# Emptying a product's PSUM banks ahead of the next product's low parts, and eight banks in turn

## The chip, the cores and the metric

The kernel runs on one core of a Trainium2 chip. Its engines work side by side, each through its own queue in order: TensorE (PE in the profile; its weight loads are PEld), VectorE (DVE), ScalarE (ACT), GpSimd (POOL) and SyncE (SP), which here issues transfers. The metric is the device time of one execution in microseconds. Before the change three runs took 3308.37, 3308.54 and 3318.48 us.

## The reference

One decoder layer for a prompt of 512 tokens and 8 sample tokens (520 columns together), width 2048. Cut to the matrix products that matter here:

```
h   = modulate(rmsnorm(x, norm1_g), shift1, scale1)
rkv = h @ w_in                          # 2048 -> 6144, then attention and RWKV-7 on the halves
x   = x + gate1 * (concat(att, rwkv) @ w_out)              # 2048 -> 2048
h2  = modulate(rmsnorm(x, norm2_g), shift2, scale2)
gate, up = split(h2 @ w_gu)                                # 2048 -> 2 x 5632
x   = x + gate2 * ((silu(gate) * up) @ w_down)             # 5632 -> 2048
```

All of it is float32.

## The kernel before

**A product.** Every large matrix product is cut into products of 256 output rows. `product` (line 133) makes one of them with a seven-multiplication block scheme: for each pair of 128-row blocks of the input (a block of x, prepared once by `act_blocks`, line 109) it forms seven combinations of the four 128x128 weight blocks and multiplies them with seven combinations of the four blocks of x, and keeps seven sums M1 to M7. Each sum has 260 columns and fills one PSUM bank; the order of work is M1, M2, M6, M7, M4, M5, M3. There are eight banks. Seven belong to the seven sums by name, one each, so that M2 of a product must wait until M2 of the product before has been read; the eighth is for transposes.

**Float32 from two parts.** TensorE gets each operand as a high part, the value rounded to its fast 32-bit format, and a low part, the remainder. For each x block the weights go this way: SP loads them (line 130), two x blocks to a transfer pair and a buffer, with two such buffers (`RAW=2`); VectorE forms the combinations (lines 143 to 145, once for two x blocks); ScalarE casts the high part (line 149); VectorE subtracts it for the low part (line 150); TensorE does three matmuls for each of the seven sums: high by high, high by low, low by high (line 90, called by `mm`). These 21 matmuls on one x block are called a pass here. A product has eight passes in the input projection, the output projection, gate and up, and five or six in down. The high and low parts have three buffers (`HL=3`), so ScalarE can fill the fourth pass's only when TensorE is done with the first's.

**The sums.** `combine` (line 158) adds the seven banks up to the 256 x 520 result. ScalarE copies M1 (line 163), then VectorE adds M2 (line 164), M6 (165), M7 (166), subtracts M4 (167), adds M5 twice (168, 169) and M3 (170). A bank is free when its last reader is done.

**Stages.** The input projection and the mixers run to about 1471 us, the output projection (products o0 to o7) to 1708, gate and up (for u = 0 to 21 a gate product g and an up product u in turn, 44 in all) to 2715, and down to the end. After g comes a tanh (line 1419) and a product on VectorE (line 1420); after u a multiplication (1422) and a store to DRAM (1423). Down runs over four groups of 5, 6, 6 and 5 blocks; each reads the stored results back, prepares its x blocks and makes eight products (d00 to d07 for the first group), whose results are added to y on VectorE (lines 1440, 1445, 1446). In the last group the finished y is also transposed by TensorE through the eighth bank and stored.

**Order.** The program is traced in the order of the text. A planner then orders each engine's queue by a simulated timeline: of the instructions whose inputs and buffers it takes to be ready, the one traced first goes first. On the chip each engine follows that order, and waits where something is late.

Of the kernel before, what the change touches and what calls it, by code (L numbers as in the profile page):

```python
# [8 lines left out]
F32 = mybir.dt.float32  # L9
# [69 lines left out]
def hymba_step(tc, a):  # L79
# [17 lines left out]

    def strassen(mkpool, sfx, ht, NX=8, RAW=2, HL=3, PC=2, PT=1, S4="ps", placed=None):
        wf, xp, tp, sm_, pt_ = placed or [mkpool(n + sfx) for n in ("wts", "x", "tmp")] + [None, None]
        sm_, pt_, turn_ = sm_ or tp, pt_ or tp, [0]  # L100
        psF, psG = mkpool("ps" + sfx, space=PSUM, side="left"), mkpool("px" + sfx, space=PSUM, side="right")

        def psf(name, tag="ps"):
            return (psG if tag == "ps" else psF).tile([P, 512], F32, tag=tag, name=name, bufs=1)

# [67 lines left out]
        return tp, wf, xp, psF, psf, pair_tile, act_blocks, columns, product, combine  # L173

    from contextlib import ExitStack

    with ExitStack() as top:
# [19 lines left out]
        def tr(out, in_, n=P):  # L197
            pe.transpose(out, in_=in_, identity=ident[:n, 0:n])  # L198
# [67 lines left out]
        pha = mid.enter_context(ExitStack())  # L266
        tp, wf, xp, psF, psf, pair_tile, act_blocks, columns, product, combine = strassen(lambda name, **kw: pools(pha)(name, **{"side": RIGHT, **kw}), "a", HS, PC=3)

# [560 lines left out]
        with ExitStack() as wk_stack:  # L829
# [497 lines left out]


        yp, xC, pt_, tmp_, xA, sB, wts_, xB, xD = [pool(n + "f") for n in ("y", "xc", "pt", "tmp", "xa", "small", "wts", "xb", "xd")]
        xpool = (xA, xA, xB, xB, xC, xC, xC, xD)  # L1330
        tp, wf, xp, psF, psf, pair_tile, act_blocks, columns, product, combine = strassen(
            pool, "f", HT, placed=(wts_, xpool, tmp_, sB, pt_), PT=2, S4="pt")
        NRAW = NRAWF
# [47 lines left out]
        nt = [slice(b * P, min(b * P + P, TOK)) for b in range(5)]  # L1381
        po = psF.tile([P, 512], F32, tag="M1", name="n2", bufs=1)
        for b, t_ in enumerate(nt):
# [8 lines left out]
        ve.tensor_tensor(rd, ident.unsqueeze(1).to_broadcast([P, 5, P]), rt[:, 1].unsqueeze(2).to_broadcast([P, 5, P]), op=ALU.mult)  # L1392
        rs2 = [psF.tile([P, 512], F32, tag=order[1 + i], name=f"rs2{i}", bufs=1) for i in range(2)]
        mm(rs2[0], ones, rd[:, :4].rearrange("p b t -> p (b t)"))
# [31 lines left out]
        YD = 2  # L1426
        for gi, (p0, p1) in enumerate(groups):
# [6 lines left out]
            for u in range(KT // 2):  # L1434
                c = combine(product(columns(w_down[:, u * 256 : (u + 1) * 256]), kp, xs, f"d{gi}{u}"), f"d{gi}{u}")
                f2 = slice(2 * u, 2 * u + 2)
                for j in range(2):
                    f = 2 * u + j
                    if j < YD:
                        ve.scalar_tensor_tensor(y[:, f, :SEQ], in0=c[:, j, :SEQ], scalar=modT[:, 48 + f, 0:1], in1=y[:, f, :SEQ],  # L1440
                                                op0=ALU.mult, op1=ALU.add)
                    else:
                        ac.mul(c[:, j, :SEQ], c[:, j, :SEQ], modT[:, 48 + f, 0:1])
                        gp.tensor_add(y[:, f, :SEQ], y[:, f, :SEQ], c[:, j, :SEQ])
                ve.tensor_mul(c[:, :, SEQ:], c[:, :, SEQ:], modT[:, 48 + 2 * u : 50 + 2 * u, 1:9])
                ve.tensor_add(y[:, f2, SEQ:], y[:, f2, SEQ:], c[:, :, SEQ:])
                if gi == len(groups) - 1:
                    ot = pair_tile(f"ot{u}", "pt").rearrange("p a t -> p (a t)")[:, :1024].rearrange("p (b c) -> p b c", b=4)
                    for j in range(2):
                        f = 2 * u + j  # L1450
                        pt = psf(f"pyt{f}")
                        for b in range(4):
                            tr(pt[:, b * 128 : (b + 1) * 128], y[:, f, b * 128 : (b + 1) * 128])
                        ac.copy(ot[:, :, j * 128 : (j + 1) * 128], pt.rearrange("p (b e) -> p b e", b=4))
                    sp.dma_start(a["y_prompt"][0].rearrange("(b p) d -> p b d", p=P)[:, :, u * 256 : (u + 1) * 256], ot)
        ys = [pair_tile(f"ys{i}").rearrange("p a t -> p (a t)")[:NB, :1024] for i in range(2)]
        for i in range(4):
            pt = psF.tile([P, 512], F32, tag=order[i], name=f"pys{i}", bufs=1)
            for j in range(4):
# [34 lines left out]
```

## Time and profile before

| | |
|---|---|
| median of three runs | 3308.54 us (3308.37 to 3318.48) |
| the profiled execution | 3317.61 us, its span 3315.8 us |
| TensorE busy (matmuls / weight loads) | 2895.7 / 2576.9 us |
| VectorE busy | 2486.4 us |
| ScalarE busy | 1275.8 us |
| GpSimd busy | 203.5 us |
| mean granted TensorE clock | 0.915 of full speed |
| transfers | 476.19 MB |

The span is from the first to the last instruction of the profiled execution. Busy times are unions of the instructions' durations; matmuls overlap one another, so a busy TensorE is not one at its peak. The share of a whole span hides the stages, which have different limits.

### The profile page before, as it was taken

How to read it: one execution, taken by the hardware profiler on the slowest of the kernel's cores; microseconds unless marked ns; L12 is line 12 of the kernel's file. 1: busy time of each engine (PE TensorE's matmuls, PEld its weight loads, DVE VectorE, ACT ScalarE, POOL GpSimd, SP SyncE). 2: the span in 40 equal slices, each digit the busy share in tenths (PEclk: the TensorE clock that was granted, in tenths of full speed). 3: DMA queues.
4: the chain of work that ended last, by engine and by line, in shares of the span. 5: the costliest groups of instructions: out<-in, count | busy, mean ns of one | idle time of the engine just before them, and what ended most of it. 6: DMA issues, size and time to landing. Idle time of an engine off the chain costs nothing.

```text
span 3315.8 us, 59346 instructions
## 1 busy us (share of the span) xinstructions
PE 2895.7 (87%) x23474; PEld 2576.9 (78%) x23474; DVE 2486.4 (75%) x4888; ACT 1275.8 (38%) x2047; POOL 203.5 (6%) x216
## 2 busy tenths in 40 slices
PE   6798999789979699868959999999999987888988
PEld 3577888688946466648859999999999987887887
DVE  6866788777757576657787878777777788889886
ACT  3443443333424244543443333333333343334333
POOL 0100111110010221110000000000000000000000
PEclk8889999889968798869979999999999999999989
DMA  8656666544389895443313333333333332323223
GB/s 272 228 179 211 191 209 199 181 134 135 116 258 295 243 256 136 117 121 109 109 38 99 112 109 109 109 109 103 109 103 115 103 131 93 111 88 115 90 96 103
DMA packets 460443, 476.19 MB, mean 144 GB/s; under 512 B 83070, under 2 KB 384083, under 8 KB 460164
## 3 DMA queue, kind: packets, MB, share of 16 engines
q1 hardware_dynamic: 449984, 452.15, 43.7%
q10 hardware_dynamic: 7428, 11.65, 1.1%
q0 software_dynamic: 2752, 8.60, 0.8%
q8 instruction: 184, 3.01, 0.4%
q14 instruction: 95, 0.78, 0.1%
HBM read 409.10 MB, written 68.17 MB: 144 GB/s over the span
## 4 chain that ended last, share of the span: by engine, by line
DVE 21%; PE 19%; DMA 17%; ACT 4%; issue 4%; SPq 2%; POOL 0%; ACTq 0%; DVEq 0%; POOLq 0%
DMA raw_ada<-in_ada_w 1%; SPq L130 1%; DMA K<-in_cache_k 1%; DVE x_a L125 1%; DMA a<-actd 1%; PE pz L90 1%; PE u15M L90 1%; PE g1M L90 1%; PE ada L90 1%; PE u14M L90 1%; PE u10M L90 1%; PE g17M L90 1%; PE u11M L90 1%; PE g6M L90 1%; PE g2M L90 1%
## 5 line engine op out<-in xcount | busy, mean ns | idle before, releaser
L90 PE MATMUL ada<-raw_ada,c_st 128*32 128x512 f32 x448 | 80.9, 760 | 24.4 <-DMA raw_ada<-in_ada_w 23.8
L1266 POOL TENSOR_TENSOR K<-K,qb 128x1024 f32<-128x1024 f32 (+2 forms) x24 | 58.5, 2447 | 125.4 <-DMA K<-in_cache_k 99.9
L1217 ACT ACTIVATE z<-z,mx 128x128 f32<-128x128 f32 (+3 forms) x64 | 35.8, 559 | 74.6 <-DVE mx L1216 37.8
L1066 ACT ACTIVATE Sall<-pch,ppl 64x64 f32<-64x64 f32 x128 | 39.4, 308 | 57.4 <-PE pch L90 52.6
L90 PEld LDWEIGHTS pg<-AR,BK 64*128 64x128 f32 x256 | 41.5, 238 | 23.4 <-DVE GM L925 8.1
L90 PE MATMUL pg<-AR,BK 64*128 64x128 f32 x256 | 50.1, 344 | 10.2 <-DVE GM L925 6.3
L90 PE MATMUL pz<-ak,aq 64*128 64x256 f32 (+3 forms) x128 | 56.0, 565 | 3.4 <-DVE at L1235 2.9
L198 PE MATMUL pzt<-ident,z 128*128 128x128 f32 x160 | 36.6, 334 | 20.2 <-ACT z L1219 15.6
L1213 DVE SCALAR_TENSOR_TENSOR z<-pz,rnq,T 128x128 f32<-128x128 f32 (+3 forms) x64 | 34.6, 543 | 23.9 <-PE pz L90 22.7
L90 PE MATMUL g0M<-x_g,g0hl 128*128 128x260 f32 x168 | 33.7, 369 | 19.4 <-ACT x_g L124 6.4
L198 PEld LDWEIGHTS pzt<-ident,z 128*128 128x128 f32 x160 | 20.6, 162 | 37.6 <-ACT z L1219 18.2
L90 PEld LDWEIGHTS ada<-raw_ada,c_st 128*32 128x32 f32 x448 | 11.0, 120 | 49.8 <-DMA raw_ada<-in_ada_w 37.7
L90 PE MATMUL o0M<-x_m,o0hl 128*128 128x260 f32 x168 | 32.5, 360 | 18.1 <-ACT x_m L124 14.4
L90 PEld LDWEIGHTS g0M<-x_g,g0hl 128*128 128x128 f32 x168 | 30.0, 263 | 23.0 <-ACT x_g L124 7.7
L90 PEld LDWEIGHTS o0M<-x_m,o0hl 128*128 128x128 f32 x168 | 29.0, 254 | 21.8 <-ACT x_m L124 17.0
L1440 DVE SCALAR_TENSOR_TENSOR y<-c_d,modT,y 128x512 f32<-128x512 f32 x64 | 45.7, 748 | 0.0
L925 DVE TENSOR_TENSOR GM<-pg,cst 128x512 f32<-128x512 f32 x32 | 21.9, 685 | 31.3 <-PE pg L90 31.2
L90 PE MATMUL ao<-adr,c_st 128*32 128x256 f32 x384 | 31.7, 402 | 14.5 <-DMA adr<-in_ada_w 11.1
L1267 DVE TENSOR_REDUCE lg<-K 128x16 f32<-128x1024 f32 (+2 forms) x24 | 29.1, 1213 | 20.4 <-POOL K L1266 20.3
L90 PE MATMUL ada<-xb,c_st 128*32 128x512 f32 x128 | 22.0, 765 | 25.2 <-DMA xb<-in_ada_w 19.9
L90 PE MATMUL po<-zt,av 128*64 128x128 f32 x320 | 40.7, 314 | 0.4 <-ACT zt L1229 0.3
L1219 ACT ACTIVATE z<-z,mx 128x128 f32<-128x128 f32 (+3 forms) x64 | 35.5, 560 | 9.6 <-DVE mx L1218 8.9
(2111 smaller groups left out, 9087.8 us busy)
## 6 DMA issues: line engine op xcount, KB each, us to landing
raw_ada<-in_ada_w SPq DMA_DIRECT2D x56, 1024.0 KB
adr<-in_ada_w SPq DMA_DIRECT2D x48, 512.0 KB
xb<-in_ada_w SPq DMA_DIRECT2D x16, 1024.0 KB
actd<-c_u SPq DMA_DIRECT2D x22, 520.0 KB
a<-actd SPq DMA_DIRECT2D x22, 520.0 KB
lsd<-lx SPq DMA_DIRECT2D x12, 520.0 KB
prd<-rkv SPq DMA_DIRECT2D x24, 256.0 KB
K<-in_cache_k SPq DMA_DIRECT2D x16, 384.0 KB
```

The costliest lines, as they stand in the source:

```text
L90: pe.matmul(out, lhsT=lhsT, rhs=rhs, start=start, stop=stop)
L125: ve.tensor_sub(x[:, 1, o:e], src, x[:, 0, o:e].bitcast(F32))
L130: sp.dma_start(raw.rearrange("p (k m) c -> p k (m c)", k=2), src[k * P : (k + 2) * P, :].rearrange("(k p) m -> p k m", p=P))
L198: pe.transpose(out, in_=in_, identity=ident[:n, 0:n])
L925: ve.tensor_tensor(GM[i][:, :, :, h], pg, gmask.unsqueeze(2).to_broadcast([P, 2, 2, P]), op=ALU.mult)
L1066: ac.activation(S[hb[h], ch + 1, hb[h]], pc_[hb[h], ch, :], AF.Copy, scale=ppl[hb[h], pr, ch : ch + 1])
L1213: ve.scalar_tensor_tensor(z, in0=pzs[h][:, :nk], scalar=rn[:, qi, h : h + 1], in1=Ts[h][:, 384 - 128 * qi :], op0=ALU.mult, op1=ALU.add)
L1217: ac.activation(z, z, AF.Exp, bias=mx[:, 0:1], accum_out=mx[:, 1:2])
L1219: ac.activation(z, z, AF.Copy, scale=mx[:, 2:3])
L1266: OK.tensor_mul(K[:n], K[:n], qb[:n])
L1267: ve.tensor_reduce(lg[:n, i, :], K[:n].rearrange("p (g e) -> p g e", e=E), axis=AX.X, op=ALU.add)
L1440: ve.scalar_tensor_tensor(y[:, f, :SEQ], in0=c[:, j, :SEQ], scalar=modT[:, 48 + f, 0:1], in1=y[:, f, :SEQ], op0=ALU.mult, op1=ALU.add)
```

## The change

It has three parts. In every product the low parts of the second and third x block (i = 1 and 2) are queued on VectorE behind the last sum of the product that was combined before (`tc.issue_after`: order of issue alone, no waiting for its end). From the second normalization on, all PSUM tiles come from one pool of eight banks with one name, taken in turn, so that a product's M1 gets the bank that its predecessor did not use; the pools of the output projection are closed for that. And the VectorE work behind a product in gate, up and down (lines 1420, 1422 with its store, and down's additions with the last group's transposes) is collected in a list `after` and traced behind the second x block of the next product. The branch for `j >= YD`, which was never taken, is dropped.

```diff
-        psF, psG = mkpool("ps" + sfx, space=PSUM, side="left"), mkpool("px" + sfx, space=PSUM, side="right")
+        psF, psG = (ppool or mkpool)("ps" + sfx, space=PSUM, side="left"), (ppool or mkpool)("px" + sfx, space=PSUM, side="right")
+
+        ring = []
 
         def psf(name, tag="ps"):
+            if ring:
+                return ring[0].tile([P, 512], F32, tag="m", name=name, bufs=8)
             return (psG if tag == "ps" else psF).tile([P, 512], F32, tag=tag, name=name, bufs=1)
...
+        held, after = [None], []
+
         def product(load, kpairs, xs, name, hook=None):
 
+            prev, held[0] = held[0], None
             M = {m: psf(f"{name}{m}", m) for m in order}
...
                     ac.copy(w[:, 0], tw[:, j, 1:])
-                    ve.tensor_sub(w[:, 1], tw[:, j, 1:], w[:, 0].bitcast(F32))
+
+                    with tc.issue_after(prev) if i in (1, 2) and prev is not None else nullcontext():
+                        ve.tensor_sub(w[:, 1], tw[:, j, 1:], w[:, 0].bitcast(F32))
                     for m in order:
...
                     if hook:
                         hook()
+                    while i == 1 and after:
+                        after.pop(0)()
             return M
...
-            ve.tensor_add(q[1, 1], q[1, 1], v["M3"])
+            held[0] = ve.tensor_add(q[1, 1], q[1, 1], v["M3"]).ins
             return c
...
+        ps_out.close()
+        ring.append(pool("ring", space=PSUM))
+        po = psf("n2")
...
-            ve.scalar_tensor_tensor(g, in0=th, scalar=1.0, in1=g, op0=ALU.add, op1=ALU.mult)
+
+            def gate(g=g, th=th):
+                ve.scalar_tensor_tensor(g, in0=th, scalar=1.0, in1=g, op0=ALU.add, op1=ALU.mult)
+
+            after.append(gate)
             v = combine(product(columns(w_gu[:, DFF + u * 256 : DFF + (u + 1) * 256]), kp_g, xs, f"u{u}", hook=fill_f(1)), f"u{u}")
-            ve.tensor_mul(v, v, g)
-            sp.dma_start(actd[u], v)
+
+            def gated(u=u, g=g, v=v):
+                ve.tensor_mul(v, v, g)
+                sp.dma_start(actd[u], v)
+
+            after.append(gated)
+        while after:
+            after.pop(0)()
...
+                def add(gi=gi, u=u, c=c):
+                    f2 = slice(2 * u, 2 * u + 2)
+                    for f in (2 * u, 2 * u + 1):
+                        ve.scalar_tensor_tensor(y[:, f, :SEQ], in0=c[:, f % 2, :SEQ], scalar=modT[:, 48 + f, 0:1], in1=y[:, f, :SEQ],
                                                 op0=ALU.mult, op1=ALU.add)
+                    ve.tensor_mul(c[:, :, SEQ:], c[:, :, SEQ:], modT[:, 48 + 2 * u : 50 + 2 * u, 1:9])
+                    ve.tensor_add(y[:, f2, SEQ:], y[:, f2, SEQ:], c[:, :, SEQ:])
...
+                after.append(add)
+        while after:
+            after.pop(0)()
```

## Rows read from the trace of the kernel before

**Rows 1.** Stretches: us; busy us and instructions by engine; clock; DMA share; GB/s.
```profile
core 0: us, PE busy (x) PEld busy (x) DVE busy (x) ACT busy (x) POOL busy (x), PEclk, DMA share, GB/s
60.00:1471.00 1411.00, 1227.97 (x10768) 988.42 (x10764) 970.75 (x2184) 559.67 (x1128) 186.57 (x185) 0.87 0.63 190
...
1777.70:2715.50 937.80, 881.97 (x7060) 859.85 (x7058) 737.01 (x1195) 343.61 (x407) 0.00 (x0) 0.99 0.34 109
2715.50:3315.80 600.30, 511.58 (x3776) 486.03 (x3776) 498.74 (x956) 216.38 (x284) 0.00 (x0) 0.94 0.31 101
...
1757.60:1777.70 20.10, 20.10 (x171) 20.10 (x170) 16.57 (x28) 8.59 (x10) 0.00 (x0) 1.00 0.33 103
```

**Rows 2.** Line 90 on TensorE, 1777.7 to 2715.5: idle us, times, by ender.
```profile
  DVE c_u L164: 18.5, 21
  DVE c_g L164: 18.2, 21
  ACT u21hl L149: 2.5, 1
```

**Rows 3.** Chain of waits, 1990 to 2030: start us, us, what.
```profile
1995.71 3.69 DMA g6w<-in_w_gu
...
1999.50 0.06 DVE g6w L143
...
2000.11 0.43 DVE c_u L164
...
2000.59 17.14 PE g6M L90 x141
```

**Rows 4.** Timeline at u5 to g6: start us, us, instruction, [idle before].
```profile
1996.75 2.09 DVE L150 TENSOR_TENSOR g6hl<-g6w,g6hl 128x896 fp32r<-128x896 f32 x2 [1.14 <-ACT g6hl L149]
...
1997.67 0.38 ACT L163 COPY c_u<-u5M 128x260 f32<-128x260 f32 x1
...
1998.19 1.09 PE L90 MATMUL g6M<-x_g,g6hl 128*128 128x260 f32 x6
1999.50 0.69 DVE L143 TENSOR_TENSOR g6w<-g6w 128x512 f32<-128x512 f32 x1 [0.66 <-DMA g6w<-in_w_gu]
2000.11 0.42 DVE L164 TENSOR_TENSOR c_u<-c_u,u5M 128x260 f32<-128x260 f32 x1
...
2000.59 15.69 PE L90 MATMUL g6M<-x_g,g6hl 128*128 128x260 f32 x129 [1.30 <-DVE c_u L164]
...
2003.77 1.08 DVE L150 TENSOR_TENSOR g6hl<-g6w,g6hl 128x896 fp32r<-128x896 f32 x1
...
2005.11 1.24 DVE L1422 TENSOR_TENSOR c_u<-c_u,c_g 128x1040 f32<-128x1040 f32 x1
...
2006.30 2.62 ACT L149 CAST g6hl<-g6w 128x896 fp32r<-128x896 f32 x3 [3.32 <-PE g6M L90]
```

**Rows 5.** Timeline at g0 to u0.
```profile
1757.57 0.43 DVE L164 TENSOR_TENSOR c_g<-c_g,g0M 128x260 f32<-128x260 f32 x1
...
1757.68 7.00 PE L90 MATMUL u0M<-x_g,u0hl 128*128 128x260 f32 x57
1757.91 0.42 DVE L165 TENSOR_TENSOR c_g<-c_g,g0M 128x260 f32<-128x260 f32 x1
1758.25 0.69 DVE L143 TENSOR_TENSOR u0w<-u0w 128x512 f32<-128x512 f32 x1
...
1761.62 0.42 DVE L170 TENSOR_TENSOR c_g<-c_g,g0M 128x260 f32<-128x260 f32 x1
```

**Rows 6.** The chain of waits in down, 2957 to 2995.
```profile
2960.06 6.43 PE d15M L90 x51
...
2967.53 3.11 DVE d15hl L150 x3
...
2971.07 3.50 DMA d16w<-in_w_down
...
2975.28 0.42 DVE c_d L164
```

More of the change, by code (lines that the diff above doesn't have):

```diff
@@ L96, in hymba_step, with strassen @@
     xsel = dict(M1=0, M2=1, M3=2, M4=6, M5=3, M6=4, M7=5)
-    def strassen(mkpool, sfx, ht, NX=8, RAW=2, HL=3, PC=2, PT=1, S4="ps", placed=None):
+    def strassen(mkpool, sfx, ht, NX=8, RAW=2, HL=3, PC=2, PT=1, S4="ps", placed=None, ppool=None):
         wf, xp, tp, sm_, pt_ = placed or [mkpool(n + sfx) for n in ("wts", "x", "tmp")] + [None, None]
         sm_, pt_, turn_ = sm_ or tp, pt_ or tp, [0]
-        psF, psG = mkpool("ps" + sfx, space=PSUM, side="left"), mkpool("px" + sfx, space=PSUM, side="right")
+        psF, psG = (ppool or mkpool)("ps" + sfx, space=PSUM, side="left"), (ppool or mkpool)("px" + sfx, space=PSUM, side="right")
+        ring = []
         def psf(name, tag="ps"):
+            if ring:
+                return ring[0].tile([P, 512], F32, tag="m", name=name, bufs=8)
             return (psG if tag == "ps" else psF).tile([P, 512], F32, tag=tag, name=name, bufs=1)
@@ L169, in combine @@
             ve.tensor_add(q[0, 1], q[0, 1], v["M5"])
-            ve.tensor_add(q[1, 1], q[1, 1], v["M3"])
+            held[0] = ve.tensor_add(q[1, 1], q[1, 1], v["M3"]).ins
             return c
-        return tp, wf, xp, psF, psf, pair_tile, act_blocks, columns, product, combine
-    from contextlib import ExitStack
+        return tp, wf, xp, psF, psf, pair_tile, act_blocks, columns, product, combine, after, ring
+    from contextlib import ExitStack, nullcontext
     with ExitStack() as top:
@@ L266, in hymba_step @@
         pha = mid.enter_context(ExitStack())
-        tp, wf, xp, psF, psf, pair_tile, act_blocks, columns, product, combine = strassen(lambda name, **kw: pools(pha)(name, **{"side": RIGHT, **kw}), "a", HS, PC=3)
+        tp, wf, xp, psF, psf, pair_tile, act_blocks, columns, product, combine, after, ring = strassen(lambda name, **kw: pools(pha)(name, **{"side": RIGHT, **kw}), "a", HS, PC=3)
         pp_ = pools(pha)("par")
@@ L1326, in hymba_step @@
         mid.close()
+        ps_out = top.enter_context(ExitStack())
         yp, xC, pt_, tmp_, xA, sB, wts_, xB, xD = [pool(n + "f") for n in ("y", "xc", "pt", "tmp", "xa", "small", "wts", "xb", "xd")]
         xpool = (xA, xA, xB, xB, xC, xC, xC, xD)
-        tp, wf, xp, psF, psf, pair_tile, act_blocks, columns, product, combine = strassen(
-            pool, "f", HT, placed=(wts_, xpool, tmp_, sB, pt_), PT=2, S4="pt")
+        tp, wf, xp, psF, psf, pair_tile, act_blocks, columns, product, combine, after, ring = strassen(
+            pool, "f", HT, placed=(wts_, xpool, tmp_, sB, pt_), PT=2, S4="pt", ppool=pools(ps_out))
         NRAW = NRAWF
@@ L1381, in hymba_step @@
         nt = [slice(b * P, min(b * P + P, TOK)) for b in range(5)]
-        po = psF.tile([P, 512], F32, tag="M1", name="n2", bufs=1)
+        ps_out.close()
+        ring.append(pool("ring", space=PSUM))
+        po = psf("n2")
         for b, t_ in enumerate(nt):
@@ L1392, in hymba_step @@
         ve.tensor_tensor(rd, ident.unsqueeze(1).to_broadcast([P, 5, P]), rt[:, 1].unsqueeze(2).to_broadcast([P, 5, P]), op=ALU.mult)
-        rs2 = [psF.tile([P, 512], F32, tag=order[1 + i], name=f"rs2{i}", bufs=1) for i in range(2)]
+        rs2 = [psf(f"rs2{i}") for i in range(2)]
         mm(rs2[0], ones, rd[:, :4].rearrange("p b t -> p (b t)"))
@@ L1435, in hymba_step @@
                 c = combine(product(columns(w_down[:, u * 256 : (u + 1) * 256]), kp, xs, f"d{gi}{u}"), f"d{gi}{u}")
[L1436 to L1440, printed above, removed]
-                                                op0=ALU.mult, op1=ALU.add)
-                    else:
-                        ac.mul(c[:, j, :SEQ], c[:, j, :SEQ], modT[:, 48 + f, 0:1])
-                        gp.tensor_add(y[:, f, :SEQ], y[:, f, :SEQ], c[:, j, :SEQ])
@@ L1445, in hymba_step @@
[L1445 to L1455, printed above, removed]
+                def add(gi=gi, u=u, c=c):
+                    f2 = slice(2 * u, 2 * u + 2)
+                    for f in (2 * u, 2 * u + 1):
+                        ve.scalar_tensor_tensor(y[:, f, :SEQ], in0=c[:, f % 2, :SEQ], scalar=modT[:, 48 + f, 0:1], in1=y[:, f, :SEQ],
+                                                op0=ALU.mult, op1=ALU.add)
+                    ve.tensor_mul(c[:, :, SEQ:], c[:, :, SEQ:], modT[:, 48 + 2 * u : 50 + 2 * u, 1:9])
+                    ve.tensor_add(y[:, f2, SEQ:], y[:, f2, SEQ:], c[:, :, SEQ:])
+                    if gi == len(groups) - 1:
+                        ot = pair_tile(f"ot{u}", "pt").rearrange("p a t -> p (a t)")[:, :1024].rearrange("p (b c) -> p b c", b=4)
+                        for j in range(2):
+                            f = 2 * u + j
+                            pt = psf(f"pyt{f}")
+                            for b in range(4):
+                                tr(pt[:, b * 128 : (b + 1) * 128], y[:, f, b * 128 : (b + 1) * 128])
+                            ac.copy(ot[:, :, j * 128 : (j + 1) * 128], pt.rearrange("p (b e) -> p b e", b=4))
+                        sp.dma_start(a["y_prompt"][0].rearrange("(b p) d -> p b d", p=P)[:, :, u * 256 : (u + 1) * 256], ot)
@@ L1456, in hymba_step @@
+                after.append(add)
+        while after:
+            after.pop(0)()
         ys = [pair_tile(f"ys{i}").rearrange("p a t -> p (a t)")[:NB, :1024] for i in range(2)]
         for i in range(4):
-            pt = psF.tile([P, 512], F32, tag=order[i], name=f"pys{i}", bufs=1)
+            pt = psf(f"pys{i}")
             for j in range(4):
```

1 line of the change is left out of this document (removed).

## The prediction

> **What bounds the kernel now.** I read the stretches first. The change touches every product of the kernel, but most of it lies in gate and up and in down, which are 937.8 and 600.3 us of the 3315.8 us span [rows 1]. In gate and up TensorE is busy 882.0 of 937.8 us and VectorE 737.0; in down it is 511.6 and 498.7 of 600.3, so there the two engines are about level. What an undisturbed product takes is also in that group: u0, which the trace shows without a pause, needs 20.10 us, that is 0.1196 us for each of its 168 matmuls. The 42 products g1 to u21 at that pace would take 42 x 20.10 = 844 us; they take 937.8, so 94 us are lost, 2.23 us a product.
>
> Next, what ended TensorE's idle time there. In each of the 42 products one wait ends with the sum of line 164: 18.5 + 18.2 = 36.7 us [rows 2]. The largest wait for a high part (line 149) is 2.5 us, in u21. Idle time understates the loss, since it counts from the modelled end of the last matmul. In g6 six matmuls start at 1998.19; at 0.12 us each the seventh would start at 1998.91, but starts at 2000.59 [rows 4], 1.68 us late against 1.30 us of idle time shown. With 0.38 us added for each of 42, the wait costs 36.7 + 16.0 = 52.7 us.
>
> The chain of waits says what is behind line 164: a weight transfer of 3.69 us, line 143 on it, line 164, and then TensorE [rows 3]. The timeline tells it as VectorE's queue [rows 4]. The seven sums of u5 could begin at 1998.05, when ScalarE has copied M1 (line 163, 1997.67 + 0.38). But ahead of them VectorE has two low parts of g6 (line 150, 2.09 us from 1996.75), then waits 0.66 us for the transfer that line 143 needs, then does line 143. Line 164 starts at 2000.11, 1.92 us after g6's first matmul, and its bank is the one M2 of g6 writes. The six matmuls that ran before it are M1 of the first pass and M1 of the second, drawn ahead because no other bank was free. A pass is the 21 matmuls on one block of x, 2.51 us.
>
> That has a second effect. With two passes interleaved, the first ends late, so ScalarE gets a buffer for the fourth high part only at 2006.30, 8.1 us after the product began and after 3.32 us of idle time ended by TensorE [rows 4]. From that follow the low parts, the release of the weight buffer, the next transfer of 3.7 us, and line 143 of the next boundary: a loop that closes on itself in about 21.5 us.
>
> **The change part by part.** *The order.* The low parts of the second and third pass (i = 1 and 2) issue after the seventh sum of the product before; that of the first pass stays free. It adds no instruction. Behind the held-back low part stands TensorE: in its plain order the second pass needs the low part after 21 + 2 matmuls, 23 x 0.1196 = 2.75 us after the product begins. If the planner draws the 14 matmuls of the second pass that use high parts alone ahead, 37 matmuls or 4.4 us; with the third pass's too, 6.1 us.
>
> When is it there? Line 164 follows line 165 by 0.34 us in u0 [rows 5], so seven sums take 2.35 us bare; u0 shows them with lines 143 to 145 between them, 1757.57 to 1761.95, 4.4 us. The low part adds about 1.05 (half of 2.09 in [rows 4]). If line 164 starts 0.1 us ahead of the product's first matmul, as in u0, the low part is ready at 3.3 to 5.35 us; against a need at 4.4 that costs 0 to 1.0 us. If line 164 still stands behind line 143 and its transfer and starts at 1.92 as now, it is ready at 5.3 to 7.4. I take a start in the middle, at 0.5, and the low part at 3.9 to 5.95 us, so 0 to 1.6 us and 0.8 in the middle. This takes the place of 1.68. The bounds of this term are 0 and 2.6 us a product (5.3 against a need at 2.75).
>
> *The ring.* M1 of the next product takes the eighth bank, M2 the bank of M1 (free once line 163 has copied it), M6 that of M2, and so on. M6 is needed 0.72 us after the start and each next bank 0.36 us later, while the sums free one each 0.34 us: with VectorE on time, TensorE no longer waits for a bank, and the passes need not be interleaved, which shortens the loop above. What u0 shows with seven banks is the lower bound: sums from -0.11 us on, the transfer of line 143 long there, 57 matmuls without a break [rows 5], the whole product 20.10 us. So 20.10 + 0.8 + 0.3 (0.3 for the waits for high parts, which stay; an estimate, five times u21's 2.5 us over 42 products) = 21.2 a product, 890 us in all, and 47 us gained. Both ends: 20.4 a product gives 81 gained; 20.1 + 2.6 + 0.3 = 23.0 gives 28 lost.
>
> The Trainium skill speaks against the ring. "TensorE: Matmul & The Clock Gate", in its section on HAM oscillation, reports a kernel where a second set of PSUM buffers "gave no further gain", and the section after it a kernel that cycles through the banks and loses clock between groups. By the first the ring alone would be worth nothing; by the second it would cost clock. The trace agrees with neither so far as it goes: the 42 pauses at banks here cost time while the granted clock is 0.99 [rows 1].
>
> *The deferred work.* The product gate (line 1420) and the multiply (line 1422, 1.24 us [rows 4]) move behind the second pass of the next product, and with them the store of line 1423 on SP's queue; down's four additions to y move likewise. Nothing reads the results within a product: the store of u is read only in down, y only at the end. I cost this at 0; VectorE's spare time hides it (737 of 937.8 busy). If that cover is gone, it is 1.24 us in front of line 143 of the second weight pair, once in each product.
>
> *Down.* The same order and ring. Its chain goes through 51 matmuls (6.43 us), a high part, three low parts (3.11), a transfer (3.50) and then line 164 [rows 6]; the ring lets the first pass end sooner, which shortens the first link. VectorE's 498.7 busy us are the floor, so at most 101.6 can be won. Against that, the second low part now comes after line 170: if TensorE waits for one more low part in each product it is 32 x 1.05 = 34 lost. I take 0.3 us a product, 10 gained, nearer to nothing since VectorE is nearly full.
>
> *Earlier stages.* The order also holds for the 24 products of the input projection and the 8 of the output projection, which have no ring. TensorE needs the sums there first anyway, so at most one low part is late or one sooner at each boundary: 31 x 1.05 = 33 us either way. I take 0.2 us lost each, 6 us.
>
> *The sum.* 47 + 10 - 6 = 51 us. From the profiled execution's 3317.6 us that leaves 3266.6. The median of the runs is 3308.5, 9.1 us below that execution, so the forecast is 3257.5, rounded to **3258**.
>
> **The rivals.**
> *The wait changes its name.* TensorE's pause moves from line 164 to the second pass's low part, about 1.7 us as before, because VectorE has the same work in the same 6 us. For it: VectorE is busy without a break from 1999.50 to the low part at 2003.77 [rows 4]. Against it: a fifth of VectorE's time is free and u0 shows room. Then down and the rest cancel, too: 3300 to 3317, about 3308.
>
> *VectorE sits on line 143 with everything behind it (slower).* The planner saw line 143 ready before line 164 (that is the order now). With the low part barred, line 143 and its two followers come straight after the first low part, and VectorE waits there for the transfer. Line 164 starts at 1.92 as before, but the low part at 4.3 or later, ready at 5.3: 2.55 us against the 1.68 lost now, 0.87 x 42 = 37, and 6 more from the earlier stages: 3352. It decides from the point where the transfer lands later than some 0.7 us after the product's start; now line 143 starts 1.31 after it in g6. Against it: with the first pass ending sooner the transfer is issued sooner.
>
> *The clock falls.* If handing banks round made the clock of gate and up what down has now, 0.94 for 0.99 [rows 1], TensorE would lose 5% of 938 us, 47 us: 3355 with nothing gained. The pauses get shorter, not longer, so this is unlikely. It is the Trainium skill's second case above.
>
> *u0's pace everywhere.* 81 us in gate and up and 1 us a product in down, 32: 113 less, 3195.
>
> **How the numbers follow.** The forecast 0.55, its own range 3230 to 3290; the wait that changes its name 0.17; VectorE on line 143 0.16; the clock 0.03; u0's pace 0.09. This kernel's runs tell 0.3%, about 10 us, from no change. Faster by more than that: 0.55 + 0.09 + 0.02 of the second case = 0.66; within it 0.13; slower 0.16 + 0.03 + 0.02 = 0.21. The range that leaves out 2 in 10 reaches from most of the fast case to a little past the unchanged one: 3205 to 3325.
>
> **What would show it.** In the changed profile line 164's share of TensorE's idle time in gate and up should fall from 36.7 us to under 10, and waits for line 150 rise to some 20 to 30. On VectorE at a boundary the seven sums stand before the second low part; line 164 starts within 0.7 us of the product's first matmul. The first pass ends before 6 us, and the idle time before line 143 shrinks. Gate and up should be near 890 us, down near 590, the part to 1471 us within some 20 us of its length. I am wrong if line 164 still starts 1.5 us late, if the wait for line 150 takes 1.7 us or more in a product, or if the gain in gate and up is lost in the first 1471 us.

## The result, and the profile after

The changed kernel takes 3407.07 us (median of 4 runs, 3394.28 to 3412.40) against 3313.51 us for the kernel before on the same chip (3308.37 to 3322.96): a ratio of 1.027 [1.024, 1.030]. It is slower by some 94 us, where 51 us faster was forecast. The rival named as the slower one came about, and with it a second cost that no case held: the low part that was held back also holds a weight buffer.

In the changed file VectorE's combinations are lines 150 to 152 (143 to 145 before), the high cast 156 (149), the low part 159 (150), the copy of M1 174 (163), the seven sums 175 to 181 (164 to 170), the product gate 1437, the multiply 1443, and SP's load 134 (130).

The stretches of the changed kernel, with the columns of [rows 1]:

```profile
core 0: us, PE busy (x) PEld busy (x) DVE busy (x) ACT busy (x) POOL busy (x), PEclk, DMA share, GB/s
60.00:1489.00 1429.00, 1238.68 (x10768) 991.16 (x10764) 970.59 (x2183) 558.31 (x1128) 191.01 (x185) 0.86 0.62 188
...
1797.80:2786.70 988.90, 902.53 (x7058) 866.69 (x7057) 743.46 (x1192) 340.06 (x406) 0.00 (x0) 0.99 0.32 103
2786.70:3404.00 617.30, 514.72 (x3779) 484.32 (x3777) 501.12 (x960) 217.24 (x286) 0.00 (x0) 0.95 0.30 98
```

Against [rows 1], gate and up went from 937.8 to 988.9 us, down from 600.3 to 617.3, and the output projection begins at 1490 us in place of 1472. That is 51 + 17 + 18, and 2 between them: the 88 us by which the span grew. VectorE's work did not grow (737 to 743 us in gate and up) and the clock there is 0.99 as before. So time was lost in waiting.

TensorE's idle time in gate and up by what ended it, the answer to [rows 2] (us, times; the largest groups):

```profile
  DVE c_g L175: 9.8, 19
  ACT c_g L174: 9.6, 18
  ACT u21hl L156: 2.7, 1
  DVE g14hl L159: 2.5, 2
```

The wait for the first sum fell, from 36.7 us to 9.8 for the sums of gate products and almost none for those of up. A wait for ScalarE's copy of M1 came, since with the ring M2 takes the bank that this copy frees; ring and deferral without the order show no such wait, so the ring by itself does not bring it. The rest is spread over single products' high and low parts, so I added it up by place. For the 42 products I took each pair of successive matmuls of a product that start more than 0.15 us apart and counted what exceeds 0.118 us, by the pass in which the late matmul stands (by its number, 21 to a pass). What a lower clock adds is counted with the waits. The last row is an experiment of the next section, the changed kernel without the order:

| us over 42 products | 1st pass | 2nd | 3rd | 5th | 7th | gate and up |
|---|---|---|---|---|---|---|
| before | 68.9 | 3.1 | 0 | 0 | 16.1 | 937.8 |
| after | 65.6 | 26.8 | 0 | 48.4 | 2.1 | 988.9 |
| ring and deferral alone | 4.9 | 2.6 | 19.1 | 0 | 34.8 | 905.2 |

Against the kernel before, the first two passes lose 92 us where they lost 72, and the fifth, which is the first to use the third pair of weights, loses 48 where it lost nothing. In the seventh 14 us come back. Against the same kernel without the order the picture is another: the order costs 85 us in the first two passes and 48 in the fifth, and 52 come back in the third and seventh. What ring and deferral had won in the first two passes, the order took away again.

The timeline of the changed kernel at u5 to g6, the boundary of [rows 4] (start us, us, instruction, idle before):

```profile
2029.81 0.65 PE L90 MATMUL g6M<-x_g,g6hl 128*128 128x260 f32 x4
2031.01 0.69 DVE L150 TENSOR_TENSOR g6w<-g6w 128x512 f32<-128x512 f32 x1 [3.38 <-DMA g6w<-in_w_gu]
2031.62 1.08 DVE L159 TENSOR_TENSOR g6hl<-g6w,g6hl 128x896 fp32r<-128x896 f32 x1
...
2032.76 13.51 PE L90 MATMUL g6M<-x_g,g6hl 128*128 128x260 f32 x98 [2.31 <-DVE g6hl L159]
2032.96 0.42 DVE L175 TENSOR_TENSOR c_u<-c_u,u5M 128x260 f32<-128x260 f32 x1
...
2035.50 0.42 DVE L181 TENSOR_TENSOR c_u<-c_u,u5M 128x260 f32<-128x260 f32 x1
2035.83 2.09 DVE L159 TENSOR_TENSOR g6hl<-g6w,g6hl 128x896 fp32r<-128x896 f32 x2
2036.98 0.88 SPq L134 DMA_DIRECT2D g6w<-in_w_gu  x2
...
2040.52 0.69 DVE L150 TENSOR_TENSOR g6w<-g6w 128x512 f32<-128x512 f32 x1 [0.35 <-DMA g6w<-in_w_gu]
```

Read it down VectorE's queue. At 2031.01 it has stood 3.38 us on line 150, the second pair's combination, whose transfer is not there. Behind it wait the first low part (2031.62, which nothing bars), then the seven sums (2032.96 to 2035.92), then the two held low parts. TensorE had four matmuls to do and idled 2.31 us. From 2034.4 to 2037.6 its granted clock was 0.51, the lower of its two levels, so part of the 98 matmuls that follow are slow as well. Only when the held low part of the second block is done, 7.2 us after the product began, does SP issue the third pair's load (2036.98): that low part is the last reader of the first of the two weight buffers.

In g6 the third pair is just in time. In 36 of the 42 products the fifth pass starts late and the wait ends with the cast of a high part; g15 is one of those with the longest wait (timeline from 2460 to 2474):

```profile
2462.27 0.88 SPq L134 DMA_DIRECT2D g15w<-in_w_gu  x2
...
2467.57 0.69 DVE L150 TENSOR_TENSOR g15w<-g15w 128x512 f32<-128x512 f32 x1 [2.21 <-DMA g15w<-in_w_gu]
...
2469.34 1.78 ACT L156 CAST g15hl<-g15w 128x896 fp32r<-128x896 f32 x2 [6.54 <-DVE g15w L152]
...
2470.34 3.93 PE L90 MATMUL g15M<-x_g,g15hl 128*128 128x260 f32 x19 [1.91 <-ACT g15hl L156]
```

The chain of waits from the boundary u5 to g6 on (start us, us, what), against [rows 3], where it passes through a transfer once and then stays on TensorE for 17.14 us:

```profile
2026.47 4.45 DMA g6w<-in_w_gu
2031.01 0.69 DVE g6w L150
...
2035.91 1.01 DVE g6hl L159
2036.98 0.37 SPq L134
2037.39 3.01 DMA g6w<-in_w_gu
2040.52 0.70 DVE g6w L150
...
2044.29 0.68 DVE g6w L150
2044.97 1.00 DVE g6hl L159
2045.97 0.35 DVE g6w L151
2046.41 4.41 DMA u6w<-in_w_gu
2050.91 0.69 DVE u6w L150
```

TensorE is not in it at all. Combination, sums, low part, release of a buffer, load, transfer, combination: here a loop between VectorE and the transfers sets the pace, with a cast of ScalarE's (0.95 us) between the rows shown.

### The profile page after: what moved, and what is told of

Read it like the earlier page. It is cut to its first block, busy times and chain, and to the rows that moved or that the text cites. A ratio compares the mean times of both kernels' runs of the same rounds, so it can differ in the third digit from the quotient of the medians.

```text
span 3404.0 us, 59433 instructions
## 1 busy us (share of the span) xinstructions
PE 2930.7 (86%) x23474; PEld 2586.0 (76%) x23474; DVE 2496.7 (73%) x4888; ACT 1273.0 (37%) x2047; POOL 208.0 (6%) x216
## 3 DMA queue, kind: packets, MB, share of 16 engines
q1 hardware_dynamic: 449984, 452.15, 42.7%
q8 instruction: 184, 3.01, 0.4%
## 4 chain that ended last, share of the span: by engine, by line
DVE 26%; DMA 19%; PE 6%; issue 4%; ACT 2%; SPq 1%; DVEq 0%; ACTq 0%; POOL 0%; POOLq 0%
SPq L134 1%; DVE x_a L129 1%; DVE y L1464 1%; DVE c_g L1437 1%; DMA a<-actd 1%; DMA mix<-mixd 0%; DMA g0w<-in_w_gu 0%; PE d05M L90 0%; DVE x_g L129 0%; PE o1M L90 0%; PE d03M L90 0%; DMA u6w<-in_w_gu 0%; PE o0M L90 0%; DMA d13w<-in_w_down 0%; DMA d02w<-in_w_down 0%
## 5 line engine op out<-in xcount | busy, mean ns | idle before, releaser
L1228 ACT ACTIVATE z<-z,mx 128x128 f32<-128x128 f32 (+3 forms) x64 | 35.9, 561 | 93.0 <-DVE mx L1227 58.3
L90 PE MATMUL pz<-ak,aq 64*128 64x128 f32 (+3 forms) x128 | 60.0, 591 | 1.0 <-DVE z L1224 0.9
L128 ACT CAST x_a<-s_a 128x1040 fp32r<-128x1040 f32 x22 | 23.3, 1060 | 50.5 <-DVE s_a L125 50.5
```

What stands on the lines that cost most here:

```text
L90: pe.matmul(out, lhsT=lhsT, rhs=rhs, start=start, stop=stop)
L128: ac.copy(x[:, 0, o:e], src)
L1228: ac.activation(z, z, AF.Exp, bias=mx[:, 0:1], accum_out=mx[:, 1:2])
```

## The experiments

Stage times are from each run's profiled execution, one for each kernel; ratios are against the kernel before on the same chip. The runs are on several chips, where the kernel before takes from 3313.51 to 3334.41 us, so an expected time is read by its distance from that. "Free" means that no low part is held.

**One part at a time.** The order alone (no ring, nothing deferred), the ring alone, the deferral alone, and ring and deferral without the order:

```diff
-with tc.issue_after(prev) if i in (1, 2) and prev is not None else nullcontext():
+with tc.issue_after(prev) if False and prev is not None else nullcontext():   # not in the order alone
-        ps_out.close()
-        ring.append(pool("ring", space=PSUM))         # taken out in the order alone, the deferral alone
-            after.append(gate)
+            gate()                                    # likewise gated, add: the order alone, the ring alone
```

> The order alone: low parts 1 and 2 held behind the sums, seven named banks, nothing deferred. Theory (the held low part is late, so its weight buffer and its transfer are late): most of the 93 us loss, 3380 to 3410, with the 18 us before the output projection in it. Rival (the ring makes M2 wait for ScalarE's copy of M1): within 15 us of before. Rival (the deferred work lies in VectorE's chain): within 15 us of before.

> The eight banks in turn alone: no low part held, nothing deferred. Theory: no loss, 3295 to 3320, since the wait for line 164 only moves by one bank. Ring rival: slower by 20 to 40 us, in gate and up, with TensorE waiting for ScalarE's copy of M1.

> The deferred work alone: line 1420, the multiply and down's additions behind the second pass of the next product; no low part held, seven named banks. Theory: 3300 to 3320. Deferral rival: slower by 20 us or more.

> The changed kernel without the order (no low part held): ring and deferral stay. Theory: the loss is gone, 3290 to 3320, and the first 1471 us are as before. Both rivals: 3340 or more, the order being innocent.

| | median us | ratio | gate and up |
|---|---|---|---|
| order alone | 3429.41 | 1.028 [1.026, 1.030] | 995.1 |
| ring alone | 3355.78 | 1.006 [1.004, 1.008] | 905.8 |
| deferral alone | 3337.25 | 1.001 [0.999, 1.003] | 945.5 |
| ring and deferral | 3299.19 | 0.988 [0.986, 0.991] | 905.2 |

The kernel before takes 3331.23 us on this chip. The order alone has the whole loss, with 42.7 us at the fifth pass. The ring wins 32 us in gate and up, but alone it missed its expectation: the last group of down takes 191.9 us against 147.1 before. The transposes of the finished y now take banks of the ring at the boundary, and TensorE waits 53.0 us in front of them for VectorE's additions to y, against 1.1 before. The deferral, worth nothing alone, moves them out of the way: with both, that wait is 2.8 us and the group takes 146.8. Together they beat the kernel before, by more than expected:

```profile
1784.90:2690.10 905.20, 873.65 (x7052) 856.72 (x7051) 726.61 (x1187) 339.51 (x403) 0.00 (x0) 1.00 0.36 112
```

**Which low part.** Ring and deferral stay; `i == 2`, then `i == 1` alone is held; then `i == 1` behind the third sum in place of the seventh.

```diff
-with tc.issue_after(prev) if i in (1, 2) and prev is not None else nullcontext():
+with tc.issue_after(prev) if i == 1 and prev is not None else nullcontext():
```

> The changed kernel with only the third block's low part (i = 2) held behind the seventh sum; the second's is free again. Theory (the held low part i = 1 is what costs: it keeps the first weight buffer, so the third pair's transfer is issued some 6.5 us later, and the sums stand behind the second pair's transfer): 3285 to 3315 us, ratio 0.985 to 0.995, gate and up near 905 us, as with nothing held. Rival (any low part behind the sums is late for TensorE): half of the changed kernel's loss stays, 3340 to 3380 us, gate and up 930 to 960.

> The changed kernel with only the second block's low part (i = 1) held. Theory: all of the loss is here: 3385 to 3415 us, ratio 1.02 to 1.03, gate and up 980 to 995. Rival (each held low part costs its share): 3340 to 3380 us, gate and up 930 to 960.

> Ring and deferral; only the second block's low part is held, and behind the third sum (M7) in place of the seventh: four sums, about 1.4 us, sooner. If the loss grows with the time that the low part is held (theory): about halfway between nothing held (gate and up 905 us) and held behind the seventh (1004): 930 to 970 us, ratio 1.005 to 1.025. If any hold costs the whole (rival): 985 to 1005 us, ratio over 1.03.

Holding `i == 2` gave 0.993 [0.990, 0.995] and 901.3 us in gate and up, as with nothing held: that low part came behind the sums anyway. Holding `i == 1` gave 1.037 [1.032, 1.042], 1004.5 us and 46.5 us at the fifth pass, more than expected and more than with both held; why is not settled. Behind the third sum it gave 1.017 [1.013, 1.021]; the fifth pass lost 19.5 us, but gate and up took 987.8, above the 930 to 970 expected. So the second block's low part carries the loss, and the longer it is held the later the third pair: its load goes out 0.97 us after the product's first matmul with nothing held, 4.26 behind the third sum, 6.68 behind the seventh.

**Is it the transfer ahead of the sums?** The second pair's combinations are queued behind the seventh sum as well, first with both low parts held, then with them free.

```diff
-                ve.tensor_sub(tw[:, :, 4:6], ...)
+                with tc.issue_after(prev) if i0 == 2 and prev is not None else nullcontext():
+                    ve.tensor_sub(tw[:, :, 4:6], ...)          # and the two that follow
```

> The changed kernel, and the combinations of the second weight pair (lines 150 to 152 at i0 = 2) are queued behind the seventh sum too, so that no transfer stands ahead of the sums. If the loss comes from the sums' standing behind that transfer (the prediction's slower rival): the first sum starts within 0.7 us of the product, the held low part runs at 3 to 4 us in place of 5.8, the third pair's transfer is issued near 4 us in place of 7.2, and most of the loss goes: gate and up 890 to 925 us, 3290 to 3330 in all. If a held low part i = 1 is late enough for the first weight buffer wherever the sums stand (rival): gate and up stay over 960, 3370 to 3410.

> The changed kernel with no low part held, but with the second pair's combinations held behind the sums. Theory: like the same kernel without that hold (3299 us on the other chip, ratio 0.988), or a little better, as the sums no longer wait for the transfer at all: ratio 0.980 to 0.990, gate and up 890 to 905. Rival (the second pair's later combinations delay its high and low parts, which TensorE needs 5 us after the product's start): gate and up 910 to 940, ratio 0.99 to 1.005.

Ratios 1.045 [1.038, 1.051] and 1.054 [1.049, 1.059]: both missed. With the low parts held, the first sum starts 0.57 us ahead of the product's first matmul in the mean (2.07 behind it in the changed kernel), the third pair's load goes out at 3.34 us (6.16), and the first two passes and the fifth no longer wait. But the third pass loses 115 us. Gate and up take 968.3 us, 21 less than in the changed kernel and still over the 960 of the expectation's rival; the rest of the loss is in the other stages (down takes 648 us). One boundary shows why the third pass waits:

```profile
2058.31 1.08 DVE L160 TENSOR_TENSOR g6hl<-g6w,g6hl 128x896 fp32r<-128x896 f32 x1
2059.31 0.68 DVE L151 TENSOR_TENSOR g6w<-g6w 128x512 f32<-128x512 f32 x1
...
2059.91 1.23 DVE L1444 TENSOR_TENSOR c_u<-c_u,c_g 128x1040 f32<-128x1040 f32 x1
...
2061.51 0.43 DVE L153 TENSOR_TENSOR g6w<-g6w 128x256 f32<-128x256 f32 x1
2062.10 1.79 ACT L157 CAST g6hl<-g6w 128x896 fp32r<-128x896 f32 x2 [6.57 <-DVE g6w L153]
...
2063.09 1.95 PE L90 MATMUL g6M<-x_g,g6hl 128*128 128x260 f32 x14 [1.43 <-ACT g6hl L157]
```

The second pair's combinations end at 2061.94, so the high part of the third pass comes at 2063.05, 6.6 us after the product's start; two passes take 5.0. The deferred multiply (line 1444 here, 1.23 us) stands between them. The transfer ahead of the sums is real, but putting the sums first only makes the combinations the late work. With free low parts the planner also put the third pair's combinations between those of the second; gate and up took 1037.5 us at a granted clock of 0.93, and the third pass lost 178 us, lower clock included, which says little about the order of the change.

**Is it the third pair's late transfer?** Free low parts, but from gate on the third pair's load waits for a one-element write that VectorE does behind the seventh sum.

```diff
+                if i0 == 4 and sfx == "f":
+                    with tc.issue_after(prev) if prev is not None else nullcontext():
+                        ve.memset(tw[0:1, 0, 0, 0:1], 0.0)
+                        ve.memset(tw[0:1, 1 % nb, 0, 0:1], 0.0)
```

> No low part is held; ring and deferral stay; but from gate on the third weight pair's transfer waits for a one-element write that VectorE does behind the seventh sum, so it is issued about 5 us after the product's start in place of about 1. Its output is the reference's. Theory (of the changed kernel's excess in gate and up, 48 us stand at the fifth pass, where the third pair is first used, because its buffer is given back late): TensorE waits at the fifth pass again, 30 to 60 us over the 42 products, almost none at the first two; gate and up 930 to 965 us, ratio 0.999 to 1.015. Rival (that wait comes from VectorE's being full, not from the transfer): the fifth pass stays under 10 us and gate and up near 905, ratio 0.985 to 0.995.

1.043 [1.039, 1.047], gate and up 1053.2 us. The fifth pass waits again, 108.4 us, with no low part held. The first pass lost 90.1, which the theory did not have: the planner, seeing the loads late, put the second pair's combination ahead of the first low part. So this run shows that a late load makes the fifth pass wait, not how much of the 48.4 us it is. It shows too that the combination can get ahead of the sums with no low part held: the first sum came 2.86 us after the product's first matmul.

**A third weight buffer** takes the release out of the loop. The room for it is there if the eighth block of x is left out of the output projection, gate and up, so four kernels have seven passes and leave that block's share out of their results: with the order and without, with two buffers and with three, one run each.

```diff
-        kp_g = list(range(0, KT, 2))
+        kp_g = list(range(0, KT - 2, 2))              # and kp_o without its last entry
-            pool, "f", HT, placed=(...), PT=2, S4="pt", ppool=pools(ps_out))
+            pool, "f", HT, placed=(...), PT=2, S4="pt", ppool=pools(ps_out), NX=7, RAW=3)   # or RAW=2
```

> The changed kernel with the eighth block of x left out in the output projection and in gate and up (seven passes a product, which frees the room for a third weight buffer elsewhere); two weight buffers. Bare, 42 products of seven passes take 42 x 17.6 = 739 us. Theory: waits at the fifth pass as with eight passes, 20 to 60 us over the 42 products; gate and up 810 to 880 us. Rival (the fifth pass waits only because of the eighth): under 10 us there.

> The same with three weight buffers, so that the third pair's transfer doesn't wait for the held low part. Theory (the late release makes the fifth pass wait): the fifth pass's waits fall under 10 us, and gate and up gain 20 to 60 us against two buffers; what stays is at the first two passes. Rival (VectorE is full there): the fifth pass waits as before and gate and up gain under 10 us.

> Seven passes, two buffers, no low part held. Theory: 30 to 90 us less in gate and up than with the order and two buffers; no wait at the fifth pass. Rival: within 15 us of it.

> Seven passes, three buffers, no low part held. Theory: within 15 us of two buffers without the order, since there the first buffer comes back in time; so three buffers against two are worth more with the order than without. Rival (a third buffer simply helps any order): as large a gain as with the order.

The stretch of gate and up with the order, first two buffers, then three:

```profile
1776.30:2652.40 876.10, 786.81 (x6174) 760.26 (x6174) 676.72 (x1149) 306.56 (x364) 0.00 (x0) 0.98 0.33 104
```

```profile
1756.60:2526.40 769.80, 754.60 (x6170) 743.56 (x6169) 665.23 (x1138) 310.69 (x359) 0.00 (x0) 1.00 0.37 117
```

The fifth pass's wait goes from 39.5 us to nothing and gate and up win 106 us, more than the 20 to 60 expected, down to 31 over the bare 739. Of the 106 us 57 had stood ahead of the products' first matmul. Without the order it is 875.3 and 824.9 us, a gain of 50. So two more expectations missed: the third buffer helps free low parts too, and with two buffers the order cost nothing here (without it, too, 52 us stand ahead of the products' first matmul, and 12.7 at the fifth pass; with eight passes the changed kernel has 2 ahead; why is not settled). With three buffers the order is 55 us faster than none. The whole kernels took 3265.06 us with the order and two buffers, 3086.93 with three; without it 3250.10 and 3138.40.

**The same with all eight blocks.** The room comes from two edits: the seventh combination is written over the first raw block, so that a buffer holds seven blocks, and one spare pair tile goes.

```diff
-                tw = wf.tile([P, 2, 8, P], F32, tag="raw", ...)
+                tw = wf.tile([P, 2, 7, P], F32, tag="raw", ...)
-                ve.tensor_sub(tw[:, :, 7], tw[:, :, 3], tw[:, :, 6])
+                ve.tensor_sub(tw[:, :, 0], tw[:, :, 3], tw[:, :, 6])        # wsel, lines 156 and 159 follow
-            pool, "f", HT, placed=(...), PT=2, S4="pt", ppool=pools(ps_out))
+            pool, "f", HT, placed=(...), PT=1, S4="pc", ppool=pools(ps_out), RAW=3)
```

> The changed kernel, all eight blocks, with three weight buffers in the output projection, gate, up and down (each buffer holds seven blocks in place of eight: the seventh combination is written over the first raw block; and one spare pair tile is dropped). Theory (the order was right and the two weight buffers made it dear): no wait at the fifth pass; gate and up 860 to 900 us as 42 x 20.1 bare and some 0.7 a product, down 560 to 590; 3150 to 3220 us, ratio 0.950 to 0.972. Rival (seven passes were a special case of the pairs, three and a half of them): gate and up over 940, ratio over 0.995.

> The same three buffers without the order. Theory (the order is worth something once the transfers no longer depend on it): 20 to 60 us slower than with the order, gate and up 890 to 940, ratio 0.965 to 0.990. Rival (the buffer alone is the gain): within 10 us of the kernel with the order.

With the order 3269.90 us, 0.986 [0.984, 0.989]; without it 3295.23 us, 0.994 [0.992, 0.996]. The intervals are apart: with three buffers the order wins. Its gate and up and down, then the same two without the order:

```profile
1802.30:2697.20 894.90, 865.81 (x7057) 853.35 (x7057) 729.44 (x1181) 349.38 (x401) 0.00 (x0) 1.00 0.36 112
2697.20:3278.60 581.40, 515.57 (x3779) 488.50 (x3777) 502.31 (x967) 223.62 (x290) 0.00 (x0) 0.91 0.32 106
```

```profile
1773.80:2694.40 920.60, 878.47 (x7058) 858.46 (x7058) 729.19 (x1180) 342.95 (x401) 0.00 (x0) 1.00 0.34 109
2694.40:3284.30 589.90, 515.48 (x3779) 487.81 (x3777) 501.29 (x968) 221.74 (x290) 0.00 (x0) 0.92 0.32 104
```

Gate and up and down came as expected, the whole did not (3150 to 3220). Its parts did not add up to it: with the 1778 us ahead of g1 in the kernel before, they give 3198 to 3268, and here 1802 us stand there, since the part ahead of the output projection is long again (below). In down the first product of each group, which waits for its x blocks, takes 28 to 34 us in place of 19 to 23 (26 to 37 without the order; that the missing pair tile does it is not shown).

Against the kernel with two buffers and nothing held, these two say less. Ring and deferral alone took 897 to 905 us in gate and up in the three kernels that have the same code there, and 0.988 [0.986, 0.991] and 0.991 [0.988, 0.993] for two of them as a whole. So in gate and up three buffers without the order (920.6 us) are slower than two, and the order with three buffers (894.9 us, 0.986) is not shown to be faster than no order with two. With three buffers the order still loses 47 us in the first two passes, but only 1 at the fifth and nothing in the third and seventh.

The boundary u5 to g6 with the order and three buffers:

```profile
2012.57 0.69 DVE L150 TENSOR_TENSOR g6w<-g6w 128x512 f32<-128x512 f32 x1 [1.75 <-DMA g6w<-in_w_gu]
...
2013.46 10.81 PE L90 MATMUL g6M<-x_g,g6hl 128*128 128x260 f32 x88
2013.64 0.42 DVE L175 TENSOR_TENSOR c_u<-c_u,u5M 128x260 f32<-128x260 f32 x1
...
2016.18 0.42 DVE L181 TENSOR_TENSOR c_u<-c_u,u5M 128x260 f32<-128x260 f32 x1
2016.52 2.09 DVE L159 TENSOR_TENSOR g6hl<-g6w,g6hl 128x896 fp32r<-128x896 f32 x2
...
2017.67 0.88 SPq L134 DMA_DIRECT2D g6w<-in_w_gu  x2
```

It is the changed kernel's order, but the combination that waits for its transfer ahead of the sums is the third pair's, which TensorE needs ten us later, and the load behind the held low part is the fourth pair's. TensorE does 88 matmuls without a break.

**The earlier stages, and down.** The order only in the input and output projections; and ring and deferral in gate and up only, with down as before.

```diff
+with tc.issue_after(prev) if i in (1, 2) and sfx == "a" and prev is not None else nullcontext():   # the first
+        ps_ring.close()                               # the second: the seven named banks and the eighth for down
+            add()
```

> The order only in the 32 products of the input and output projections, none from gate on; ring and deferral stay. Prediction's term for it: 6 us lost against the same kernel without the order, either way up to 33. What the four profiles with a held low part there say against the four without: 10 to 25 us lost, ratio 0.990 to 0.998. Rival (the longer first part of the changed kernel's profile is scatter between executions): ratio 0.985 to 0.991.

> No low part held; ring and deferral in gate and up alone, down with the seven named banks and the eighth, and nothing deferred, as before. Theory (ring and deferral win some 32 us in gate and up and lose some 10 in down): gate and up 900 to 908 us, down 595 to 605 in place of 610, 3275 to 3290 us, ratio 0.983 to 0.990. Rival (down's loss is not from the ring or the deferral): the same as with them in down, ratio 0.988 to 0.993.

The first gave 0.999 [0.997, 1.002], where its twins without the order or with `i == 2` alone gave 0.988 and 0.993, so the order costs there too. (`sfx == "a"` is the input projection alone; the output projection belongs to the other set, so this run has it in 24 products and not in 32.) The profiles agree: the output projection starts at 1490 to 1519 us in the eight kernels that hold the second block's low part behind the seventh sum from the start, at 1467 to 1489 in the ten with nothing or only `i == 2` held, 26 us apart in the mean. The second gave 0.991 [0.988, 0.993]: gate and up 897.1 us, but down 610.2 although its code is that of before. Its expectation missed, and why down takes 600 us in one kernel and 610 in the other is not settled.

## Why the prediction was wrong

*What bounds the kernel* held: the wait behind line 164 and the loop over the transfers, both as in [rows 3, 4]. *The ring* did most of what was said of it: with the deferral, and without the order, gate and up came to 905.2 us at a granted clock of 1.00, where it took 937.8 at 0.99 before and the forecast for all three was 890. What it left is waits for high and low parts in the third and seventh pass, 54 us or 1.3 a product, where the term for waits of that kind was 0.3. The Trainium skill's "TensorE: Matmul & The Clock Gate" reports, in its section on HAM oscillation, a kernel to which a second set of PSUM buffers "gave no further gain". In this case's traces more room in the banks gave 32 us, so they do not agree with it. *The deferral* costs nothing, as said (1.001), but its cover was wrongly named: with the ring it is what keeps down's transposes from the banks.

*The order* is the step that failed. Its term, 0.8 us a product, was for the wait for the second pass's low part, and that wait came to 26.8 / 42 = 0.6 us. But the forecast let the first pass lose nothing and put no wait on the third weight pair. The first pass lost 65.6 / 42 = 1.6 us a product and the fifth 48.4 / 42 = 1.2. There are two reasons.

I took line 164 to start 0.5 us after the product's first matmul, the middle between u0's start and the present one. In the mean over 42 products:

| us after the product's first matmul | first sum | second block's low part | third pair's load |
|---|---|---|---|
| before | 1.67 | -0.26 | 0.85 |
| after | 2.07 | 5.01 | 6.16 |
| ring and deferral, free | 0.87 | -0.14 | 0.97 |
| order, three buffers | 1.11 | 3.99 | -3.68 |

The first sum came later, not sooner, since with the low part held the planner put the combination with its transfer ahead of everything, the product's own first low part included (that one ran 1.27 us ahead of the first matmul in the mean before, and 0.20 behind it after; by what ended its waits, TensorE lost some 24 us to it in the first pass and some 28 to banks). That is the rival that I gave 0.16, and its point of decision was passed: the transfer landed 1.1 us after g6's start, against the 0.7 that I set, and the combination started 0.79 after the start in the mean. Its low part was ready at 5.3 us; measured, it was ready at 6.1.

And I said that the ring would shorten the loop, without following the held low part around it: moved by 5.3 us, it gives the first weight buffer back 5.3 us later. With a transfer (3.01 us in g6) and the combinations behind it, the third pair then comes late for the fifth pass. The prediction had this link ("the low parts, the release of the weight buffer, the next transfer") and priced it only in the other direction.

So the order, which was to bring a wait of 1.68 us down to 0.8, cost (988.9 - 905.2) / 42 = 2.0 us a product against ring and deferral alone. The rival's 3352 was short as well: its 37 us for gate and up stand against 20 in the first two passes and 48 in the fifth, with 14 back in the seventh; and its 6 for the earlier stages against some 26 (18 between the two profiles of before and after). Where in the input projection those are lost is open; the bound that I worked out, 33 either way, holds the mean.

*Down* was to gain 10 us and lost 17. Of these 12 are there without the order (612.3 us with ring and deferral), and 10 in a kernel whose down is as before (610.2), so the cause stays open.

*The clock* was no cause of any size: 0.99 in gate and up as before, 0.95 in down against 0.94. By the trace's clock records it stood at the lower level for 27 us of gate and up where it had for 17, which is some 5 us of TensorE's work (an estimate, at half the speed). *What would show it*: of the signs of being wrong, "line 164 still starts 1.5 us late" is the one that came.

## What to carry to other kernels

Before an instruction on an in-order engine is held back, ask what it frees: as the last reader of a buffer it sets the next transfer, and a few us there outweigh the wait that the hold removes. With eight passes the order lost 84 us in gate and up with two weight buffers and won 26 with three, so test an order together with the buffers that it leans on. Then compare with leaving the order alone: two buffers and no order (0.988) are not shown to be slower than three buffers with it (0.986). Whether a combination that waits for a transfer goes ahead of the instructions that free PSUM depends on when TensorE needs each: ahead of them, the second pair's held up the sums; behind them, it came too late for the third pass (115 us).

## What was not expected of the hardware

Nothing in the engines' own times: the low part took 1.08 us, a sum 0.42 and a matmul 0.12 before and after. What was new is the planner's, not the chip's: how much its order moves when one instruction is barred. The second pair's combination went ahead of a low part that nothing barred. It did so as well where only a load was late, so that the bar alone does it is not shown.
